# Fourteen pairs of expert chunks as seven block products instead of eight, in the second matmul of a PEER layer

## The chip, the core and the metric

The kernel runs on one core of one Trainium2 chip. The metric is the device time of that core in microseconds (us). A measurement is the median of several executions, and the traced execution has its own time.

The engines are named as in the profile: PE is TensorE (matmuls), PEld its weight loads, DVE is VectorE, ACT is ScalarE, POOL is GpSimd, and SP is SyncE, whose queue issues nearly all DMA loads. Each engine takes its instructions in the order in which they stand. An instruction that waits for a semaphore holds everything behind it on its engine.

## The reference, cut to what matters

```python
def reference(x, c, ...):                       # one layer: 256 tokens, width 1024
    mod = jax.nn.silu(c) @ ada_w + ada_b         # shift1, scale1, gate1, shift2, scale2, gate2
    ...                                          # two attention groups, w_out; x = x + g1 * y
    h2 = rmsnorm(x, norm2_g) * (1.0 + sc2) + sh2
    x = x + g2 * peer(h2, peer_wq, peer_subkeys, peer_u, peer_v)
    return rmsnorm(x, final_g)

def peer(h, wq, subkeys, u_tab, v_tab):          # 16384 experts of one neuron each
    ...                                          # product keys: 8 heads x 16 experts a token, gates by softmax
    a = h . u_tab[ids]                           # first expert matmul
    w = gates * gelu(a)
    return w . v_tab[ids]                        # second expert matmul
```

The kernel does not gather the experts. It computes all 16384 of them densely, as 128 chunks of 128 experts: with G the gates of the chosen experts spread over all experts (zero elsewhere), the second matmul is y = (G * gelu(h2 u^T)) v, of shape 256 x 16384 by 16384 x 1024.

## The kernel before, in words

All matmuls of the heavy part run as three products of split operands. A float32 operand is split into `hi`, its rounded part (an ACT copy to fp32r), and `lo`, the rest (a subtraction). `mm3` issues hi·hi, hi·lo and lo·hi into one PSUM bank (lines 130 to 133).

The work comes as a list of units, `order`, one unit of 128 x 1024 values each. For each unit `load` issues a DMA of 512 KB on SP's queue into a `raw` tile, and `split` makes `hi` on ACT and `lo` on POOL (kind "b") or DVE (kind "c"). `unit()` hands out the next unit, and prepares `lead[0]` units ahead in the program (1 here). In the last part of the kernel there are 3 `raw`, 4 `hi` and 3 `lo` tiles, used in turn. So the load of a unit waits until the unit three places before it in `raw` has been split, and a `lo` waits until TensorE has used the one three places before it.

- **First expert matmul.** 128 u chunks (24 matmuls of 256 columns each), with gelu. The results of 36 of them lie in `GA`, and the rest in `GB`, one cell of 256 tokens for each chunk. Beside 89 of them the gates are spread by one-hot matmuls (`gp`), 64 rounds.
- **Second expert matmul.** It follows without a gap. For each chunk i, `gated(i)` splits cell i into `wx` (3 tiles: ACT makes its hi half, DVE its lo half), `unit()` brings v chunk i, and `give` issues 4 products, one for each token tile T and half f of the width: 12 matmuls of 512 columns into the four PSUM banks `yp[T][f]`. The last 3 chunks are issued product by product, so that the banks become ready one after another. Two u chunks (126 and 127) stand between chunk 124 and these three.
- **Gate 2.** Its sum over the 8 row blocks of `ada` stands in the program from chunk 90 on, but the tile framework's scheduler places the loads and the sums early. They read into `GA` cells that are used up, not into `raw` (lines 859 to 873). The row then goes through DRAM (`g2d`) to be broadcast.
- **End.** y times gate 2, plus the residual stream `x1`, RMSNorm, and the store.

The order of instructions on each engine is set by the framework's scheduler, which orders them by priority and by its own estimates.

Of the kernel before, what the change touches and what calls it, by code (L numbers as in the profile page):

```python
# [15 lines left out]
D = 1024  # L16
S = 256
# [5 lines left out]
BIG = 1e30  # L23
LOW = -3e38
AHEAD = 36
BESIDE = 90
LEAD = 1
LATE = 5
E2AT = 0
HOLD = 1  # L30
GATE2 = 90
ENDLEAD = 2
LAST = 3
FG0 = (("p", 0, 512), ("p", 512, 1024))
# [36 lines left out]
def body(tc, xT, cols, ada, w_in, e2, w_out, wq, sk, u, v, fg, const, dil, out):  # L71
    nc = tc.nc
    with ExitStack() as top:
# [15 lines left out]

        def split(i, raw, eng):  # L90
            hi = room(i, "hi", F32R, *HIB)
            nc.scalar.activation(hi, raw, AF.Copy)  # L92
            lo = room(i, "lo", F32R, *LOB)
# [17 lines left out]
        order += [(v[i], "c") for i in range(AHEAD + BESIDE - 1)]  # L111
        for i in range(AHEAD + BESIDE - 1, NKEY - LAST):
            order += [(u[i + 1], "c"), (v[i], "c")]
        order += [(u[i], "c") for i in range(NKEY - LAST + 1, NKEY)]
        order += [(v[i], "c") for i in range(NKEY - LAST, NKEY)]
        ready = []
        loaded = []
# [57 lines left out]
        with ExitStack() as pre:  # L175
# [593 lines left out]
        def cell(i, t0, t1):  # L769
            return GA[:, i, t0:t1] if i < AHEAD else GB[:, i - AHEAD, t0:t1]  # L770
# [58 lines left out]
        with tc.tile_pool(name="py", bufs=1, space=bass.MemoryType.PSUM) as PY:  # L829
# [1 line left out]
            W = {}  # L831

            def gated(i):
                if i < done:
                    w = cell(i, 0, S)
                else:
                    ps = u_chunk(i)
                    w = WK.tile([128, S], F32, tag="w", name="w", bufs=1)
                    nc.scalar.activation(w, ps[:, :S], AF.Gelu)
                    nc.vector.tensor_mul(w, w, cell(i, 0, S))  # L840
# [14 lines left out]
            def used(n):  # L855

                return GA[:, 4 * n:4 * n + 4, :].rearrange("p a t -> p (a t)")

            def gate2(k):

                if k == 0:
                    nc.sync.dma_start(used(0), row(sild))
                if k < 8:
                    nc.sync.dma_start(used(1 + k % 2), ada[(40 + k) * 128:(41 + k) * 128, :])
                if k:
                    raw, c = used(1 + (k - 1) % 2), C_ADAB + 40 + k - 1
# [9 lines left out]
            for i in range(NKEY - LAST):  # L876
                gated(i + 1)
                if i >= GATE2 and (i - GATE2) % 3 == 0 and (i - GATE2) // 3 < 9:
                    gate2((i - GATE2) // 3)
                hl = unit()  # L880
                for T in range(2):
                    for f in range(2):
                        give(i, hl, T, f)

            lead[0] = ENDLEAD
            for i in range(NKEY - LAST + 1, NKEY):
# [6 lines left out]


            ys, scr = [used(T) for T in range(2)], used(2)
            g2b, fgb = used(3), used(4)
            x1 = [used(5 + T) for T in range(2)]
            for dst, src in ((g2b, row(g2d)), (x1[0], x1d[0]), (x1[1], x1d[1]), (fgb, row(fg))):
                nc.sync.dma_start(dst, src)
# [102 lines left out]
```

## Time and profile before

| what | value |
|---|---|
| median of 3 runs | 994.31 us (993.05 to 996.11) |
| the profiled execution | 996.15 us, span of its trace 994.3 us |
| PE busy | 965.2 us, 97% of the span |
| DVE busy | 724.4 us (73%) |
| ACT busy | 545.9 us (55%) |
| mean granted TensorE clock | 0.978 of full speed |

A matmul's busy time overlaps with that of the next, so the cost of one is read from the distance of the starts. A DVE or ACT instruction's time likewise overlaps a little with the next on its engine.

### The profile page before, as it was taken

The page shows a single profiled execution, that of the slowest core. Times are in us where ns is not written, and L with a number is a line of the kernel's source. Part 1 is how long each engine was busy: PE and PEld are TensorE (multiplying, and loading weights), DVE is VectorE, ACT ScalarE, POOL GpSimd, SP SyncE. Part 2 cuts the span into 40 slices and gives each one's busy share as a digit, 9 for nine tenths or more (in the row PEclk, how much of TensorE's full clock was granted, in tenths as well). Part 3 has the DMA queues.
Part 4 walks back from the last instruction along what each step waited for, and adds up shares of the span by engine and source line. Part 5 has one row for each costly group of instructions (what it writes and reads, how often), then busy time and mean ns, then how long its engine had stood idle before and what let it go on. Part 6 is the DMA issues. An engine that isn't in the chain of part 4 may idle for free.

```text
span 994.3 us, 17364 instructions
## 1 busy us (share of the span) xinstructions
PE 965.2 (97%) x6315; PEld 879.2 (88%) x6315; DVE 724.4 (73%) x1683; ACT 545.9 (55%) x1010; POOL 439.9 (44%) x201
## 2 busy tenths in 40 slices
PE   7998989999999999999999999999999999999996
PEld 4886978899999999999999999888888888888885
DVE  5969867799994577788888887677555555555555
ACT  4465556645444666666666666554545555444553
POOL 4458337587888777777777777000000000000002
PEclk8899869999999999999999999999999999999998
DMA  9687646555554555555555555688766666566662
GB/s 344 251 302 274 213 191 222 159 162 157 186 178 147 153 166 169 154 166 168 162 162 168 165 157 168 206 288 277 244 196 191 196 195 196 191 191 193 191 215 79
DMA packets 53398, 193.76 MB, mean 195 GB/s; under 512 B 5816, under 2 KB 6080, under 8 KB 53184
## 3 DMA queue, kind: packets, MB, share of 16 engines
q1 hardware_dynamic: 52672, 191.59, 59.8%
q8 instruction: 49, 0.80, 0.3%
q10 hardware_dynamic: 576, 1.05, 0.3%
q14 instruction: 37, 0.30, 0.1%
q0 software_dynamic: 64, 0.01, 0.0%
HBM read 190.52 MB, written 2.11 MB: 194 GB/s over the span
## 4 chain that ended last, share of the span: by engine, by line
PE 80%; DVE 1%; POOL 1%; ACT 1%; issue 1%; DMA 0%; POOLq 0%; ACTq 0%
PE ps L131 14%; PE ps L132 14%; PE ps L133 14%; PE y L131 12%; PE y L132 12%; PE y L133 11%; PE gp L805 3%; PE scp L660 1%; DVE xgxd L563 0%; DMA raw<-in_u 0%; POOL GA L917 0%; POOL lo L94 0%; DVE x_s L478 0%; POOL GA L923 0%; ACT xge2s L562 0%
## 5 line engine op out<-in xcount | busy, mean ns | idle before, releaser
L94 POOL TENSOR_TENSOR lo<-raw,hi 128x1024 fp32r<-128x1024 f32 x165 | 401.8, 2437 | 178.2 <-ACT hi L92 96.5
L92 ACT ACTIVATE hi<-raw 128x1024 fp32r<-128x1024 f32 x304 | 320.0, 1055 | 166.3 <-issue 63.6
L131 PE MATMUL ps<-h2h,hi 128*128 128x256 f32 x1128 | 320.4, 284 | 0.8 <-ACT GB L824 0.8
L132 PE MATMUL ps<-h2l,hi 128*128 128x256 f32 x1128 | 319.1, 283 | 0.0
L133 PE MATMUL ps<-h2h,lo 128*128 128x256 f32 x1128 | 318.8, 283 | 0.0
L94 DVE TENSOR_TENSOR lo<-raw,hi 128x1024 fp32r<-128x1024 f32 x139 | 171.9, 1237 | 136.5 <-issue 109.2
L131 PEld LDWEIGHTS ps<-h2h,hi 128*128 128x128 f32 x1128 | 216.2, 192 | 1.5 <-ACT GB L824 1.2
L132 PEld LDWEIGHTS ps<-h2l,hi 128*128 128x128 f32 x1128 | 216.4, 192 | 0.0
L133 PEld LDWEIGHTS ps<-h2h,lo 128*128 128x128 f32 x1128 | 216.2, 192 | 0.0
L131 PE MATMUL y<-hi,wx 128*128 128x512 f32 x512 | 199.2, 389 | 0.0
L133 PE MATMUL y<-hi,wx 128*128 128x512 f32 x512 | 199.2, 389 | 0.0
L132 PE MATMUL y<-lo,wx 128*128 128x512 f32 x512 | 199.2, 389 | 0.0
L873 POOL DMA_DIRECT2D g2d<-g2r x1 | 0.6, 617 | 317.0 <-ACT g2r L872 317.0
L791 DVE SCALAR_TENSOR_TENSOR gi<-iotaG,iT,gT 128x256 fp32r<-128x256 f32 x256 | 113.9, 477 | 31.5 <-PE gp L805 31.5
L131 PEld LDWEIGHTS y<-hi,wx 128*128 128x128 f32 x512 | 96.1, 188 | 20.3 <-ACT wx L843 0.2
L133 PEld LDWEIGHTS y<-hi,wx 128*128 128x128 f32 x512 | 96.1, 188 | 20.1 <-DVE wx L844 0.2
L132 PEld LDWEIGHTS y<-lo,wx 128*128 128x128 f32 x512 | 96.1, 188 | 19.6
L843 ACT ACTIVATE wx<-GB 128x256 fp32r<-128x256 f32 x90 | 37.7, 419 | 118.8 <-PE y L133 118.8
L808 DVE TENSOR_TENSOR gp<-gp,gl 128x512 f32<-128x512 f32 x64 | 44.6, 698 | 8.9 <-ACT gl L807 7.3
L788 DVE TENSOR_TENSOR jm<-iotaG,jT 128x512 fp32r<-128x512 f32 x64 | 43.6, 681 | 1.6 <-ACT iotaG L777 1.6
L811 ACT ACTIVATE GB<-gp 128x368 f32<-128x368 f32 (+31 forms) x64 | 21.3, 333 | 37.5 <-DVE gp L808 37.5
L209 DVE CUSTOM_DVE_ANT_0 araw<-araw,silb,col 128x1024 f32<-128x1024 f32 x24 | 41.4, 1738 | 0.1
(214 smaller groups left out, 1232.9 us busy)
## 6 DMA issues: line engine op xcount, KB each, us to landing
raw<-in_u SPq DMA_DIRECT2D x128, 512.0 KB, 3.6
raw<-in_v SPq DMA_DIRECT2D x128, 512.0 KB, 4.3
araw<-in_ada SPq DMA_DIRECT2D x20, 1024.0 KB, 6.2
raw<-in_w_in SPq DMA_DIRECT2D x24, 512.0 KB, 5.8
raw<-in_wq SPq DMA_DIRECT2D x16, 512.0 KB, 3.6
raw<-in_w_out SPq DMA_DIRECT2D x8, 512.0 KB, 6.4
GA<-in_ada SPq DMA_DIRECT2D x8, 512.0 KB, 5.3
e2s<-in_e SPq DMA_DIRECT2D x1, 1536.0 KB, 10.0
```

Source lines behind the costliest of these rows:

```text
L92: nc.scalar.activation(hi, raw, AF.Copy)
L94: ins = eng.tensor_tensor(lo, raw, hi.bitcast(F32), op=OP.subtract)
L131: nc.tensor.matmul(ps, wh, ah, start=first, stop=False)
L132: nc.tensor.matmul(ps, wh, al, start=False, stop=False)
L133: return nc.tensor.matmul(ps, wl, ah, start=False, stop=last)
L209: nc.vector.tensor_tensor_reduce(raw, raw, silb, 1.0, init, OP.mult, OP.add, m)
L788: nc.vector.tensor_tensor(jm, iotaG[:, None, :].to_broadcast([128, 4, 128]), jT[:, t0:t0 + 4, None].to_broadcast([128, 4, 128]), op=OP.is_ ...
L791: nc.vector.scalar_tensor_tensor(gi[:, t, :, :], iotaG[:, None, :].to_broadcast([128, 2, 128]), iT[:, t0 + t:t0 + t + 1], gT.bitcast(F32)[ ...
L805: nc.tensor.matmul(gp[:, t, :, :], jm[:, t, :], gi[:, t, :, :], start=True, stop=True)
L808: nc.vector.tensor_tensor(gp[:, :, 0, :], gp[:, :, 0, :], gl, op=OP.add)
L811: nc.scalar.activation(GB[:, m:, t0:t0 + 4], gv[:, done:, :], AF.Copy)
L843: nc.scalar.activation(wh, w, AF.Copy)
```

## The change

Two neighbouring chunks form a block matrix product: the 256 tokens are two blocks (T), the 256 experts two blocks (chunk e), the 1024 columns two blocks (f). Written out it has eight block products. Winograd's form of Strassen's scheme needs seven, at the price of sums of blocks on both sides:

- Every seventh chunk from 20 to 111 begins a pair, 14 pairs in all (`seven`). The other chunks are done as before, 5 between two pairs. Seven products of 3 matmuls of 512 columns take the place of eight.
- `pair_load` loads both v chunks (2 x 512 KB) into blocks 0 to 3 of `bl`, which is the first part of `GA`. DVE forms the sums of blocks: `pair_t13` (one subtraction of 1024 columns a partition) and `pair_t24` (two of 512). The blocks are split in four parts of 2, 1, 2 and 2 blocks (kind "s"), on ACT and DVE, and use the `hi` and `lo` tiles like any unit.
- `pair_s` forms four sums of gate blocks (128 columns each) on DVE, and splits them (`sx`). `pair_a` splits the two cells as they are (`wxh`, `wxl`).
- Products that go into one output block alone are added into `yp`. Four others have PSUM banks of their own (`P[1]`, `P[5]`, `P[6]`, `P[7]`) over all 14 pairs. After the last pair `fold` adds them up, multiplies them by gate 2 and adds them to the residual stream `x1`: 12 DVE instructions of 512 columns.
- Gate 2 is summed beside chunks 0 to 15. Its 8 row blocks are units of `order` now (kind "g"), one after every second v chunk, and take `raw` tiles.
- All 128 u chunks come before the second matmul (BESIDE 92, HOLD 3), three of them behind the last one-hot round instead of one. The loads of gate 2's row, `x1` and the final gain are issued behind the last pair in the program.

```diff
+        for i in plan:
+            order += [(p, "s") for p in range(4)] if i in seven else [(v[i], "c")]
+            if i < 16 and i % 2:
+                order.append((ada[(40 + i // 2) * 128:(41 + i // 2) * 128, :], "g"))
...
+                if kind == "s":
+                    ready.append(split(i, parts[order[i][0]], nc.vector))
+                    continue
+                if kind == "g":
+                    ready.append(load(i))
+                    continue
...
+            bl = GA[:, 0:16, :].rearrange("p (b a) t -> p b (a t)", a=2)
+            parts += [bl[:, 0:3:2, :], bl[:, 3:4, :], bl[:, 4:6, :], bl[:, 6:8, :]]
...
+            def pair_load(i):
+                for e in range(2):
+                    nc.sync.dma_start(bl[:, 2 * e:2 * e + 2, :], v[i + e].rearrange("p (f c) -> p f c", f=2))
+
+            def pair_t13(i):
+
+                nc.vector.tensor_tensor(bl[:, 4:6, :], bl[:, 1:4:2, :], bl[:, 0:2, :], op=OP.subtract)
...
+                for ops in (((a(0, 0), P[1]), (a(1, 0), yp[0][0])), ((s_(4), yp[0][1]),), ((s_(1), P[5]), (s_(3), P[7])),
+                            ((s_(2), P[6]), (a(1, 1), yp[1][0]))):
+                    hl = unit()
+                    for n, (w, o) in enumerate(ops):
+                        own = any(o is t for t in P.values())
+                        mm3(o, w[0], w[1], hl[0][:, n, :], hl[1][:, n, :], own and i == seven[0], own and i == seven[-1])
...
+            def gate2(k):
+                raw, c = unit(), C_ADAB + 40 + k
+                nc.vector.tensor_tensor_reduce(raw, raw, silr, 1.0, col[:, c:c + 1], OP.mult, OP.add, mod[:, 5, k:k + 1])
...
+                p1, r, c12, c21, c22 = (bl[:, n, :] for n in range(5))
+                nc.scalar.activation(p1, P[1], AF.Copy)
+                nc.vector.tensor_add(r, P[6], p1)
+                nc.vector.tensor_add(c12, P[5], r)
+                nc.vector.tensor_add(c21, P[7], r)
+                nc.vector.tensor_add(c22, P[7], c12)
+                for n, c in enumerate((p1, c12, c21, c22)):
+                    fs = slice(n % 2 * 512, (n % 2 + 1) * 512)
+                    nc.vector.tensor_mul(c, c, g2b[:, fs])
+                    nc.vector.tensor_add(x1[n // 2][:, fs], x1[n // 2][:, fs], c)
```

What the scheduler makes of it is seen in the order on the engines, at three places.

**SP's queue where gate 2 is loaded.** Before, the blocks of `ada` go to `GA_1996`, and the v chunks alone use `raw`:

```order
L87 DMA raw_8525<-in_v 128x1024
L87 DMA raw_8546<-in_v 128x1024
L864 DMA GA_1996<-in_ada 128x1024
L87 DMA raw_8567<-in_v 128x1024
L87 DMA raw_8588<-in_v 128x1024
L864 DMA GA_1996<-in_ada 128x1024
```

Now every third `raw` tile takes a block of `ada`. The rows are v2, v3, a block, v4, v5, a block, the first chunk of the first pair (`GA_1996`), v6, v7, a block, v8:

```order
L88 DMA raw_8460<-in_v 128x1024
L88 DMA raw_8470<-in_v 128x1024
L88 DMA raw_8491<-in_ada 128x1024
L88 DMA raw_8505<-in_v 128x1024
L88 DMA raw_8515<-in_v 128x1024
L88 DMA raw_8536<-in_ada 128x1024
L878 DMA GA_1996<-in_v 128x1024
L88 DMA raw_8550<-in_v 128x1024
L88 DMA raw_8560<-in_v 128x1024
L88 DMA raw_8581<-in_ada 128x1024
L88 DMA raw_8595<-in_v 128x1024
```

The load of an even chunk (v4, v6, v8) now waits for the split of the even chunk just before it, since the three `raw` tiles serve two chunks and a block of `ada`.

**DVE at a pair in the middle.** Before, one `lo` and one `wx` alternate through the whole second matmul:

```order
L94 TENSOR_TENSOR lo_9243<-raw_9239,hi_9241 128x1024
L844 TENSOR_TENSOR wx_9236<-GB_4125,wx_9236 128x256
L94 TENSOR_TENSOR lo_9264<-raw_9260,hi_9262 128x1024
L844 TENSOR_TENSOR wx_9257<-GB_4125,wx_9257 128x256
L94 TENSOR_TENSOR lo_9285<-raw_9281,hi_9283 128x1024
```

Now, at the third pair (chunks 34 and 35): `lo` of its first part (lo_9196), of its second (lo_9215), the lo halves of its cells (`wxl`), `lo` of its third part (lo_9225), the `wx` of the chunk behind the pair, `pair_t13` of the next pair (L882), `lo` of its fourth part (lo_9232), and `lo` of the two chunks behind it:

```order
L98 TENSOR_TENSOR lo_9196<-GA_1996,hi_9195 128x1024
L895 TENSOR_TENSOR sr_9503<-GB_4125,sr_9503 128x128
L98 TENSOR_TENSOR lo_9215<-GA_1996,hi_9214 128x512
L905 TENSOR_TENSOR wxl_9190<-GA_1996,wxh_9189 128x256 x2
L98 TENSOR_TENSOR lo_9225<-GA_1996,hi_9224 128x1024
L852 TENSOR_TENSOR wx_9211<-GB_4125,wx_9211 128x256
L882 TENSOR_TENSOR GA_1996<-GA_1996 128x1024
L98 TENSOR_TENSOR lo_9232<-GA_1996,hi_9231 128x1024
L98 TENSOR_TENSOR lo_9244<-raw_9241,hi_9243 128x1024
L98 TENSOR_TENSOR lo_9261<-raw_9258,hi_9260 128x1024
```

`pair_t13` of the next pair stands ahead of the last part of this one, and reads the next pair's two loads. On SP's queue those two loads wait for the first and the second row shown here (lo_9196 and lo_9215). This order holds at the second to the thirteenth pair. At the first pair the next `pair_t13` stands three units later, and at the last there is none.

**DVE behind the last pair.** Now: `lo` of the two chunks behind the pair, the 12 instructions of `fold` as one block with a single `wx` in it, and then `wx` and `lo` of the third chunk behind the pair. Before there was only the alternation shown above.

```order
L98 TENSOR_TENSOR lo_11015<-raw_11012,hi_11014 128x1024
L98 TENSOR_TENSOR lo_11047<-raw_11044,hi_11046 128x1024
L950 TENSOR_TENSOR GA_1996<-P6_8889,GA_1996 128x512
L852 TENSOR_TENSOR wx_11041<-GB_4125,wx_11041 128x256
L951 TENSOR_TENSOR GA_1996<-P5_8890,GA_1996 128x512
L952 TENSOR_TENSOR GA_1996<-P7_8891,GA_1996 128x512
L953 TENSOR_TENSOR GA_1996<-P7_8891,GA_1996 128x512
L956 TENSOR_TENSOR GA_1996<-GA_1996 128x512 x2
L957 TENSOR_TENSOR GA_1996<-GA_1996 128x512 x2
...
L852 TENSOR_TENSOR wx_11062<-GB_4125,wx_11062 128x256
L98 TENSOR_TENSOR lo_11068<-raw_11065,hi_11067 128x1024
```

The 12 instructions now stand between the splits of two chunks.

## Rows read from the trace of the kernel before

**Rows 1.** Windows of the second matmul: busy us (count) per engine, clock, DMA share, GB/s.
```profile
631.40:700.00 68.60, 68.60 (x305) 56.82 (x305) 48.43 (x66) 35.05 (x50) 0.00 (x0) 1.00 0.83 274
700.00:950.00 250.00, 250.00 (x1105) 206.97 (x1104) 143.78 (x185) 126.57 (x186) 0.62 (x1) 1.00 0.65 197
950.00:985.90 35.90, 35.86 (x181) 30.06 (x179) 22.03 (x29) 15.83 (x25) 2.98 (x3) 1.00 0.45 141
```

**Rows 2.** The chain that ended last, share of the span by engine.
```profile
PE 80%; DVE 1%; POOL 1%; ACT 1%; issue 1%; DMA 0%; POOLq 0%; ACTq 0%
```

**Rows 3.** Timeline of PE: start us, us, engine, line, operation, tiles.
```profile
955.31 0.39 PE L131 MATMUL y<-hi,wx 128*128 128x512 f32 x1
955.53 0.39 PE L132 MATMUL y<-lo,wx 128*128 128x512 f32 x1
...
955.99 0.39 PE L131 MATMUL y<-hi,wx 128*128 128x512 f32 x1
```

**Rows 4.** Who waited for whom, 700 to 950: us in total, times, longest.
```profile
ACT wx L843 <- PE y L133: 113.2, 85, 1.4
DVE lo L94 <- issue: 97.0, 84, 1.3
```

**Rows 5.** Groups of instructions, 631.4 to 985.9: busy us, mean ns | idle before.
```profile
L94 DVE TENSOR_TENSOR lo<-raw,hi 128x1024 fp32r<-128x1024 f32 x128 | 156.8, 1225 | 130.7 <-issue 109.2 <-ACT hi L92 15.3 <-PE ps L133 3.0
...
L867 DVE CUSTOM_DVE_ANT_0 GA<-GA,col 128x1024 f32<-128x1024 f32 x8 | 10.3, 1284 | 7.6 <-DMA GA<-in_ada 6.8 <-DVE wx L844 0.9
```

**Rows 6.** Timeline of DVE in the second matmul.
```profile
955.34 1.23 DVE L94 TENSOR_TENSOR lo<-raw,hi 128x1024 fp32r<-128x1024 f32 x1 [1.00 <-issue]
...
956.48 0.42 DVE L844 TENSOR_TENSOR wx<-GB,wx 128x256 fp32r<-128x256 f32 x1
```

**Rows 7.** DMA issues by line, windows 640 to 660 and 660 to 680: KB, us to landing.
```profile
raw<-in_v SPq DMA_DIRECT2D x7, 512.0 KB, 4.7
GA<-in_ada SPq DMA_DIRECT2D x3, 512.0 KB, 5.7
...
raw<-in_v SPq DMA_DIRECT2D x7, 512.0 KB, 5.0
```

**Rows 8.** Loads into `raw`, from 700 to 950.
```profile
DMA to landing us min/median/max: 3.4/4.3/6.1
```

**Rows 9.** Timelines of ACT and of DVE: a split whose load came late.
```profile
689.59 1.06 ACT L92 ACTIVATE hi<-raw 128x1024 fp32r<-128x1024 f32 x1 [1.17 <-DMA raw<-in_v]
690.68 1.23 DVE L94 TENSOR_TENSOR lo<-raw,hi 128x1024 fp32r<-128x1024 f32 x1 [0.67 <-ACT hi L92]
```

**Rows 10.** DVE at the end of the kernel: instructions of 512 columns.
```profile
980.65 0.69 DVE L908 TENSOR_TENSOR GA<-y,GA 128x512 f32<-128x512 f32 x1 [0.60 <-PE y L133]
981.38 0.69 DVE L909 TENSOR_TENSOR GA<-GA 128x512 f32<-128x512 f32 x1
981.99 0.68 DVE L908 TENSOR_TENSOR GA<-y,GA 128x512 f32<-128x512 f32 x1
```

**Rows 11.** The row of gate 2 to DRAM: KB, us to landing.
```profile
g2d<-g2r POOLq DMA_DIRECT2D x1, 4.0 KB, 3.7
```

**Rows 12.** Timeline of PE, earlier in the kernel, behind idle time.
```profile
97.31 0.91 PE L404 MATMUL sp<-k,q 64*128 64x256 f32 x5 [1.02 <-DVE mn L417]
130.04 0.48 PE L452 MATMUL tp<-cst,os 128*128 128x128 f32 x1 [3.19 <-ACT os L467]
159.15 0.44 PE L452 MATMUL tp<-cst,os 128*128 128x128 f32 x2 [1.31 <-ACT os L467]
```

**Rows 13.** Windows there; the clock stands after POOL's busy time.
```profile
98.00:100.00 2.00, 2.00 (x12) 1.60 (x10) 2.00 (x3) 0.84 (x1) 1.81 (x2) 0.56 0.72 289
104.00:106.00 2.00, 2.00 (x15) 2.00 (x14) 2.00 (x9) 1.42 (x6) 0.00 (x0) 0.73 0.80 236
130.00:132.00 2.00, 1.96 (x9) 1.97 (x10) 0.17 (x1) 2.00 (x8) 0.00 (x0) 0.50 0.68 188
160.00:162.00 2.00, 2.00 (x20) 2.00 (x19) 1.05 (x4) 1.39 (x3) 1.21 (x1) 1.00 0.04 8
```

More of the change, by code (lines that the diff above doesn't have):

```diff
@@ L29 @@
 E2AT = 0
-HOLD = 1
-GATE2 = 90
+HOLD = 3
+SEVEN = (20, 7, 118)
 ENDLEAD = 2
@@ L91, in split @@
             hi = room(i, "hi", F32R, *HIB)
+            lo = room(i, "lo", F32R, *LOB)
+            if raw.shape[-1] == 512:
+                n = raw.shape[1]
+                hi, lo = (t[:, :n * 512].rearrange("p (n c) -> p n c", n=n) for t in (hi, lo))
             nc.scalar.activation(hi, raw, AF.Copy)
-            lo = room(i, "lo", F32R, *LOB)
             ins = eng.tensor_tensor(lo, raw, hi.bitcast(F32), op=OP.subtract)
@@ L110, in body @@
         order += [(u[i], "b") for i in range(AHEAD + BESIDE)]
[L111 to L114, printed above, removed]
+        seven = [i for i in range(*SEVEN[:1], SEVEN[2]) if (i - SEVEN[0]) % SEVEN[1] == 0]
+        plan = [i for i in range(NKEY - LAST) if i - 1 not in seven]
+        parts = []
+        for i in plan:
+            order += [(p, "s") for p in range(4)] if i in seven else [(v[i], "c")]
+            if i < 16 and i % 2:
+                order.append((ada[(40 + i // 2) * 128:(41 + i // 2) * 128, :], "g"))
         order += [(v[i], "c") for i in range(NKEY - LAST, NKEY)]
@@ L833, in gated @@
             def gated(i):
[L834 to L840, printed above, removed]
+                w = cell(i, 0, S)
                 wx = WK.tile([128, 2, S], F32R, tag="wx", name="wx", bufs=WXB)
@@ new lines, in pair_s @@
+            def pair_s(i):
+                a11, a21, a12, a22 = (cell(i + e, T * 128, (T + 1) * 128) for e in range(2) for T in range(2))
+                sr = WK.tile([128, 4, 128], F32, tag="w", name="sr", bufs=1)
+                for o, x, y, op in ((0, a21, a22, OP.add), (2, a11, a21, OP.subtract), (1, sr[:, 0, :], a11, OP.subtract),
+                                    (3, a12, sr[:, 1, :], OP.subtract)):
+                    nc.vector.tensor_tensor(sr[:, o, :], x, y, op=op)
+                sx = WK.tile([128, 2, 4, 128], F32R, tag="gi", name="sx", bufs=2)
+                nc.scalar.activation(sx[:, 0], sr, AF.Copy)
+                nc.vector.tensor_tensor(sx[:, 1], sr, sx[:, 0].bitcast(F32), op=OP.subtract)
+                AS[i] = sx
@@ new lines, in pair_a, with pair_products, a, s_ @@
+            def pair_a(i):
+                wx = [WK.tile([128, 2, S], F32R, tag="wx", name="wx" + x, bufs=WXB) for x in "hl"]
+                for e in range(2):
+                    nc.scalar.activation(wx[0][:, e, :], cell(i + e, 0, S), AF.Copy)
+                    nc.vector.tensor_sub(wx[1][:, e, :], cell(i + e, 0, S), wx[0][:, e, :].bitcast(F32))
+                W[i] = wx
+            def pair_products(i):
+                sx, wx = AS.pop(i), W.pop(i)
+                def a(e, T):
+                    return [t[:, e, T * 128:(T + 1) * 128] for t in wx]
+                def s_(n):
+                    return [sx[:, x, n - 1, :] for x in range(2)]
+                if not P:
+                    for n in (1, 6):
+                        P[n] = PY.tile([128, 512], F32, name=f"P{n}")
+                    for n in (5, 7):
+                        P[n] = PM.tile([128, 512], F32, tag="mm", name=f"P{n}")
+                for ops in (((a(0, 0), P[1]), (a(1, 0), yp[0][0])), ((s_(4), yp[0][1]),), ((s_(1), P[5]), (s_(3), P[7])),
[4 more added lines that the diff above has]
+                        mm3(o, w[0], w[1], hl[0][:, n, :], hl[1][:, n, :], own and i == seven[0], own and i == seven[-1])
@@ L870, in gate2 @@
+            silr = WK.tile([128, D], F32, tag="gi", name="silr", bufs=2)
+            nc.sync.dma_start(silr, row(sild))
+            def gate2(k):
+                raw, c = unit(), C_ADAB + 40 + k
+                nc.vector.tensor_tensor_reduce(raw, raw, silr, 1.0, col[:, c:c + 1], OP.mult, OP.add, mod[:, 5, k:k + 1])
+                if k == 7:
+                    gp = PM.tile([128, 512], F32, tag="mm", name="gp2")
                     nc.tensor.transpose(gp[0:8, 0:128], mod[:, 5, :], ident)
@@ L873, in gate2, with fold @@
                     nc.gpsimd.dma_start(g2d, g2r)
-            gated(0)
[L876 to L879, printed above, removed]
+            g2b, fgb = used(4), used(7)
+            x1 = [used(5 + T) for T in range(2)]
+            def fold():
+                p1, r, c12, c21, c22 = (bl[:, n, :] for n in range(5))
[8 more added lines that the diff above has]
+                    nc.vector.tensor_add(x1[n // 2][:, fs], x1[n // 2][:, fs], c)
+            gated(0)
+            todo = []
+            for n, i in enumerate(plan):
+                nxt = plan[n + 1] if n + 1 < len(plan) else NKEY - LAST
+                todo += [(n + 2 if j == 0 else max(n + 2, plan.index(p) - 3 + j), j, p) for p in seven
+                         if p == next((q for q in seven if q >= nxt), None) and (i in seven or i == 16) for j in range(4)]
+                for t in [t for t in todo if t[0] <= n + 1]:
+                    todo.remove(t)
+                    (pair_load, pair_t13, pair_t24, pair_s)[t[1]](t[2])
+                (pair_a if nxt in seven else gated)(nxt)
+                if i in seven:
+                    pair_products(i)
+                    if i == seven[-1]:
+                        for dst, src in ((g2b, row(g2d)), (x1[0], x1d[0]), (x1[1], x1d[1]), (fgb, row(fg))):
+                            nc.sync.dma_start(dst, src)
+                        fold()
+                    continue
                 hl = unit()
@@ L883, in body @@
                         give(i, hl, T, f)
+                if i < 16 and i % 2:
+                    gate2(i // 2)
             lead[0] = ENDLEAD
@@ L895, in body @@
             ys, scr = [used(T) for T in range(2)], used(2)
[L896 to L899, printed above, removed]
             ssq = WK.tile([128, 4], F32, name="fssq")
```

16 lines of the change are left out of this document (6 added, 10 removed).

## The prediction

> **What bounds the kernel now.** I read the windows of the second matmul first [rows 1]. From 631.4 to 985.9 PE is busy without a break at a granted clock of 1.00, while DVE is busy 143.8 us of 250 and ACT 126.6. The chain that ended last is PE for 80% of the span [rows 2]. So in this stage time is the number of matmuls times the distance of their starts. The timeline gives that distance: 0.227 us, 0.68 us for a product of three [rows 3], 2.72 us for a chunk of four products.
>
> The other engines wait for PE: ACT for a `wx` tile that PE has used, 113 us in 250, and DVE, whose `lo` finds no free tile, for 97 us [rows 4]. They have slack, but little lead. Three `lo` tiles let the splits run two units ahead of PE. A `lo` starts when PE has used the tile three units before, that is at the end of a chunk (955.34 [rows 6], with the next chunk's first matmul at 955.31 [rows 3]).
>
> **What it removes.** 14 pairs lose one product each: 14 x 0.68 = **9.5 us**, all on the path, if PE stays fed. The rest of this part asks whether it does.
>
> **Gate 2 through `raw` (loss 8.5).** The 3 tiles serve two v chunks and one block of `ada` in turn for chunks 0 to 15. The load of an even chunk waits for the `lo` of the even chunk before it. One round is: load, from issue to landing; hi and the step to `lo`, 1.09 (689.59 to 690.68) [rows 9]; `lo`, 1.23; 0.02 to the next issue. Loads landed in 4.3 us at one in 2.72 us [rows 8], in 4.7 at ten in 20 us, and in 5.0 where they were denser [rows 7]. Three in a round of almost 7 us is one in 2.3 us, between the first two: I take 4.5. A round is then 6.84 us, and PE uses its two chunks in 5.44, so each round costs 1.4. With time 0 at the first v matmul, `lo` of v2 ends at 2.4 (its tile comes free at 0), v4's at 9.25, where PE wants it at 11.1. v6's load is issued with three others within 3 us (v5, a block, the pair's first chunk), lands 1.9 later than alone, and its `lo` ends at 18.0 instead of 16.55: 1.5 late. v8 to v16 are five rounds: 5 x 1.4 = 7.0. Sum 8.5. In the kernel before the same blocks went past `raw`, and PE did not wait [rows 1]. The sums themselves (1.28 us each [rows 5]) fit into DVE's slack.
>
> Here one rule speaks against me. The Trainium skill, page "DMA: Bandwidth & Descriptors", section "Anatomy of one DMA — SWDGE (gpsimd) path", fits a DMA's time as 2.0 us plus its bytes at 436 GB/s. For 512 KB that is 3.2 us, an estimate from that page, for another issuing path than SP's. By it a round would be 5.5 us and this term almost nothing. The rows show no load into `raw` from 700 to 950 under 3.4, and half of them over 4.3 [rows 8], so I go by the rows; the lowest of them is a rival below.
>
> **The first pair (loss 1.6).** Its `sr` tile is one with `g2r`, so DVE waits there for gate 2's row to reach DRAM: the transpose stands behind chunk 15 on PE, and the DMA lands 3.7 later [rows 11]. Behind `sr` on DVE stand the splits of v19 and of the pair, and three `sr`/`sx` sets that the scheduler moved here (some 4 us). Laid out, v19 is just in time, and the parts come 0.2, 1.0 and 0.4 late.
>
> **The pairs 2 to 13 (loss 0.87 each, 10.4).** Time 0 is the start of the pair's first part on PE; the parts start at 0, 1.36, 2.04 and 3.40. DVE's `lo` of the second part needs the tile of the chunk before last, free at -2.69; it lasts 0.69 (512 columns [rows 10]) and ends at -2.0. Only then may SP issue the next pair's second load; at 4.3 it lands at 2.3. Loads are dense here (four in 5.3 us), so 4.3 is no high value. Meanwhile DVE does `wxl`, `lo` of the third part (tile free at 0.03) and a `wx`, until 1.5, and stands at `pair_t13`, which needs that load. It lasts like `lo`, two inputs of 1024 columns, 1.15 to the next start [rows 6]. So `lo` of the fourth part starts at 3.45 and ends at 4.68. PE wants it at its third matmul of that part, 3.40 + 0.454 = 3.85 (two hi matmuls stand ahead of it there), so with the semaphore it waits 0.87. The chunk behind the pair just fits: its `lo` ends at 5.83, wanted at 5.87. DVE catches up afterwards. Its work in a period is 5 x (1.15 + 0.34) for chunks, 4.1 for the parts, 0.7 for `wxl`, 2.4 for `pair_t13` and `pair_t24`, 1.6 for the small sums: 16.2 us of a period of 18.4, so it does not bound by itself, and each pair begins the same way. A pair thus costs 0.87 and saves 0.68. If the load lands at 3.4, DVE alone sets it and the wait is 0.1; at 5.0 it is 1.6.
>
> **`fold` (loss 4.1, and 3.1 for the clock).** 12 DVE instructions, 0.61 to 0.73 each from start to start [rows 10], are 7.9 us in one block, with one `wx`. It starts 0.3 behind the last pair's end. Two chunks are split ahead and give PE 5.44. `wx` and `lo` of the third come at 9.7, wanted at 5.67: 4.1 late, once. PE was idle so long only once in the rows: 3.19 us at 130, then the clock was 0.50 [rows 12, 13]. An idle 1.31 at 159 left it at 1.00; 1.02 at 97, with little work before, was followed by half clock until about 105, some 6.2 us. For `fold` I count one such stretch, 3.1 us; below it is nothing. For the 0.9 to 1.5 of the other waits I count none.
>
> **What costs nothing.** The two u chunks moved ahead (48 matmuls) are the same work; at the end, without them, `lo` of v127 starts when v124's tile is free and ends 1.26 later, wanted at 1.59, so that cover is not missed (otherwise 1 us). POOL splits them one a chunk, as it does the 126 others. ACT has half of its time free and takes 1.5 more splits a pair. The loads of `x1`, gain and gate row are issued long before the end in both kernels. The tail is the same.
>
> **Sum.** -9.5 + 8.5 + 1.6 + 10.4 + 4.1 + 3.1 = +18.2. Against the profiled execution's 996.15 us (span 994.3) that is 1014.3; that execution lay 1.8 above the median of the runs, so on the median it is 1012.5, and I say **1012**.
>
> **The rivals.**
> - Loads land fast (not slower). At 3.4 us everywhere, a round is 5.74: the first lateness falls away, and the later rounds cost 0.9 together. The pairs cost 0.1 each, 1.2; the first pair 1.0; `fold` 4.1, with the clock 7.2. Sum +0.8, or -2.3 if the clock holds: 992 to 995. For it speaks the lowest row; against it the median [rows 8] and the denser loads [rows 7]. It decides at a landing of about 3.5. By the 3.2 of that page it would come out about 1 us lower still.
> - The clean saving: the splits keep ahead of PE at every place, and only the 9.5 counts, 985. For it speaks DVE's free time on the average [rows 1]; against it that the waits arise from the order in three places, not from DVE's sum. The largest single one, `fold`, would have to be hidden by a lead of 4 us that three `lo` tiles don't hold.
> - Contention makes it heavier. With loads at 5.0 as around 670 [rows 7], a round is 7.34: 12 us for gate 2; the pairs 12 x 1.6 = 19; the first pair 2.2; `fold` 7.2. Sum +31: 1025.
>
> **Numbers.** My forecast 0.70 (its own range 1003 to 1019), fast loads 0.15, the clean saving 0.07, contention 0.08. A measurement of this kernel can tell about 0.3%, 3 us. Faster: the clean saving, and a part of the fast loads: 0.12. Within: 0.11. Slower: 0.77. For 8 in 10 the range takes in the fast loads, and stops short of contention's end: 992 to 1021.
>
> **What would show it.** If I am right, PE has idle time of about 1.4 us before every second chunk from v6 to v16, released by DVE `lo`, whose ACT hi waited for the load; `pair_t13` waits for a load by DMA, 0.8 us at each of 12 pairs, and PE for `lo` right behind it; PE waits once about 4 us for the `wx` and `lo` behind `fold`, with the clock down afterwards. PE issues 42 matmuls of 512 columns fewer. I would be wrong if loads into `raw` land in 3.5 us or less, if `pair_t13` starts without a wait, or if the rounds of gate 2 take 5.4 us.

## The result, and the profile after

The changed kernel takes 1022.43 us (median of 4 runs, 1015.87 to 1023.19) where the kernel before takes 993.68 beside it. The ratio is 1.0274, with an interval of 1.0245 to 1.0303: slower, by 24 to 30 us. The prediction said slower, by 18. Its range ended at 1021, so the measured median lies 1.4 us above it.

The profiled execution of the changed kernel took 1022.85 us, span 1020.9, which is 26.6 more than the span before. I cut it where the work changes: the second matmul begins (639.28), the first pair (701.30), the last pair (961.39, at the end of the second window), the end of the matmuls. The windows answer to [rows 1], with the same columns (PE, PEld, DVE, ACT, POOL, clock, DMA share, GB/s):

```profile
639.30:701.30 62.00, 57.47 (x243) 44.38 (x242) 43.42 (x67) 27.82 (x44) 0.62 (x1) 1.00 0.77 250
701.30:962.00 260.70, 245.36 (x1057) 197.69 (x1056) 210.28 (x311) 153.17 (x223) 0.00 (x0) 0.99 0.57 191
962.00:985.00 23.00, 19.81 (x81) 15.88 (x80) 19.84 (x29) 11.41 (x17) 0.00 (x0) 0.93 0.40 137
985.00:1012.00 27.00, 27.00 (x121) 22.21 (x119) 17.42 (x23) 11.69 (x19) 2.19 (x2) 1.00 0.39 117
```

Before, PE was busy without a break here. Now it is idle for 4.5, 15.3 and 3.2 us in the first three windows, while DVE's share has risen to 81% in the second and is below 90% everywhere. An engine that is busy 81% of the time is no bound by itself, so what is wanted is the place of each wait. The chain that ended last (before: [rows 2]) says which engines have come into it:

```profile
PE 67%; DVE 6%; DMA 6%; ACT 2%; issue 2%; POOL 1%; POOLq 0%; DVEq 0%; ACTq 0%; SPq 0%
```

**Beside gate 2.** The same chain, piece by piece (start, us, what), from 654 to 675:

```profile
654.18 1.07 ACT hi L97
...
655.28 1.24 DVE lo L98
...
656.53 3.45 DMA raw<-in_v
...
660.00 1.07 ACT hi L97
...
661.10 1.24 DVE lo L98
...
662.35 5.31 DMA raw<-in_v
...
670.03 4.61 DMA raw<-in_v
```

Load, hi, lo, load again: PE is no longer in the chain at all. That is the ring of three `raw` tiles. PE's timeline shows where it stands, at the first and the second matmul of every second chunk:

```profile
667.67 0.39 PE L147 MATMUL y<-hi,wx 128*128 128x512 f32 x1
668.79 0.50 PE L145 MATMUL y<-hi,wx 128*128 128x512 f32 x1 [0.74 <-ACT hi L97]
670.05 0.50 PE L146 MATMUL y<-lo,wx 128*128 128x512 f32 x1 [0.76 <-DVE lo L98]
...
675.77 0.50 PE L145 MATMUL y<-hi,wx 128*128 128x512 f32 x1 [0.18 <-ACT hi L97]
677.02 0.50 PE L146 MATMUL y<-lo,wx 128*128 128x512 f32 x1 [0.76 <-DVE lo L98]
```

Two chunks take 6.98 us here (668.79 to 675.77), and 5.44 without a wait. The whole stretch from 639.28 to 701.30 holds 240 matmuls of 0.227, 54.5 us, and takes 62.0: 7.5 lost.

**A pair in the middle.** The view of waits from 701.3 to 962 (us in total, times, longest), where [rows 4] had nothing of PE or PEld:

```profile
PEld P L146 <- DVE lo L98: 21.3, 14, 3.0
...
PE P L146 <- DVE lo L98: 15.3, 13, 2.6
DVE GA L882 <- DMA GA<-in_v: 14.8, 12, 2.6
```

L882 is `pair_t13`: it waits 12 times for a load, 1.23 us each, and PE waits 13 times for a `lo`. At the fifth pair (its first matmul is at 783.09) the timelines of SP, DVE and PE give the order of it:

```profile
780.11 1.35 SPq L878 DMA_DIRECT2D GA<-in_v  x2
```

```profile
780.41 0.69 DVE L98 TENSOR_TENSOR lo<-GA,hi 128x512 fp32r<-128x512 f32 x1
...
784.27 0.42 DVE L852 TENSOR_TENSOR wx<-GB,wx 128x256 fp32r<-128x256 f32 x1
786.02 1.22 DVE L882 TENSOR_TENSOR GA<-GA 128x1024 f32<-128x1024 f32 x1 [1.33 <-DMA GA<-in_v]
787.17 1.22 DVE L98 TENSOR_TENSOR lo<-GA,hi 128x1024 fp32r<-128x1024 f32 x1
```

```profile
786.72 0.39 PE L145 MATMUL y<-hi,wxh 128*128 128x512 f32 x1
788.44 0.50 PE L146 MATMUL P<-lo,sx 128*128 128x512 f32 x1 [1.34 <-DVE lo L98]
788.78 0.40 PE L147 MATMUL P<-hi,sx 128*128 128x512 f32 x1
```

The second of the two loads goes out when `lo` of the second part is done (780.41 and 0.69, so 781.1; the row of SP merges both issues). Some 4.8 us later it has landed, and `pair_t13` starts; `lo` of the fourth part stands behind it, and PE behind that. From pair to pair (start of one to start of the next, less 81 matmuls of 0.227) the first period loses 1.1 us, the second 4.4, the third to the thirteenth 0.6 to 1.9, on average 1.41.

**`fold`.** DVE's timeline behind the last pair, and PE's:

```profile
966.70 0.68 DVE L950 TENSOR_TENSOR GA<-P,GA 128x512 f32<-128x512 f32 x1
967.30 0.41 DVE L852 TENSOR_TENSOR wx<-GB,wx 128x256 fp32r<-128x256 f32 x1
...
973.04 1.28 DVE L957 TENSOR_TENSOR GA<-GA 128x512 f32<-128x512 f32 x2
974.24 0.41 DVE L852 TENSOR_TENSOR wx<-GB,wx 128x256 fp32r<-128x256 f32 x1
974.58 1.21 DVE L98 TENSOR_TENSOR lo<-raw,hi 128x1024 fp32r<-128x1024 f32 x1
```

```profile
971.59 1.07 PE L145 MATMUL y<-hi,wx 128*128 128x512 f32 x4
975.85 0.50 PE L146 MATMUL y<-lo,wx 128*128 128x512 f32 x1 [3.19 <-DVE lo L98]
...
977.41 0.63 PE L147 MATMUL y<-hi,wx 128*128 128x512 f32 x1
977.84 0.63 PE L146 MATMUL y<-lo,wx 128*128 128x512 f32 x1
```

The block of 12, with two `wx`, holds `lo` back by 7.9 us. PE issues the four hi·hi matmuls of the chunk first, stands for 3.19, and from 976.98 to 979.97 a matmul takes 0.43 instead of 0.227. The window there has the granted clock at half (1.2 GHz), for 3.0 us, after the idle 3.19:

```profile
976.98:979.97 2.99, 2.99 (x8) 2.34 (x7) 2.18 (x4) 0.89 (x2) 0.00 (x0) 0.50 0.85 258
```

From the last pair's start to the last matmul 5.1 us are lost.

### The profile page after: what moved, and what is told of

Read it like the earlier page. It is cut to its first block, busy times and chain, and to the rows that moved or that the text cites. A ratio compares the mean times of both kernels' runs of the same rounds, so it can differ in the third digit from the quotient of the medians.

```text
span 1020.9 us, 17470 instructions
## 1 busy us (share of the span) xinstructions
PE 967.0 (95%) x6273; PEld 871.6 (85%) x6273; DVE 805.4 (79%) x1833; ACT 574.8 (56%) x1053; POOL 444.3 (44%) x203
## 4 chain that ended last, share of the span: by engine, by line
PE 67%; DVE 6%; DMA 6%; ACT 2%; issue 2%; POOL 1%; POOLq 0%; DVEq 0%; ACTq 0%; SPq 0%
PE ps L145 13%; PE ps L146 13%; PE ps L147 13%; PE y L146 7%; PE y L147 7%; PE y L145 7%; DMA raw<-in_v 4%; DVE lo L98 3%; PE gp L819 3%; PE P L146 1%; ACT hi L97 1%; PE P L147 1%; PE scp L674 1%; PE P L145 1%; DMA raw<-in_u 1%
## 5 line engine op out<-in xcount | busy, mean ns | idle before, releaser
L98 POOL TENSOR_TENSOR lo<-raw,hi 128x1024 fp32r<-128x1024 f32 x167 | 406.5, 2436 | 181.0 <-ACT hi L97 98.2
L97 ACT ACTIVATE hi<-raw 128x1024 fp32r<-128x1024 f32 x276 | 289.8, 1058 | 193.9 <-issue 63.7
L98 DVE TENSOR_TENSOR lo<-raw,hi 128x1024 fp32r<-128x1024 f32 x109 | 133.3, 1236 | 40.2 <-ACT hi L97 32.0
L146 PE MATMUL y<-lo,wx 128*128 128x512 f32 x400 | 157.9, 395 | 6.8 <-DVE lo L98 6.7
L145 PE MATMUL y<-hi,wx 128*128 128x512 f32 x400 | 156.7, 393 | 0.9 <-ACT hi L97 0.9
L147 PE MATMUL y<-hi,wx 128*128 128x512 f32 x400 | 157.0, 393 | 0.0
L146 PEld LDWEIGHTS y<-lo,wx 128*128 128x128 f32 x400 | 75.8, 189 | 26.9 <-DVE lo L98 10.0
L145 PEld LDWEIGHTS y<-hi,wx 128*128 128x128 f32 x400 | 75.7, 189 | 18.1 <-ACT hi L97 2.1
L147 PEld LDWEIGHTS y<-hi,wx 128*128 128x128 f32 x400 | 75.8, 190 | 15.4
L98 DVE TENSOR_TENSOR lo<-GA,hi 128x1024 fp32r<-128x1024 f32 (+1 forms) x56 | 60.9, 1088 | 24.9 <-PE y L146 19.9
L97 ACT ACTIVATE hi<-GA 128x1024 fp32r<-128x1024 f32 (+1 forms) x56 | 52.8, 943 | 18.8 <-PE y L147 18.8
L851 ACT ACTIVATE wx<-GB 128x256 fp32r<-128x256 f32 x70 | 27.5, 410 | 60.2 <-PE y L147 58.9
```

The costliest lines, as they stand in the source:

```text
L145: nc.tensor.matmul(ps, wh, ah, start=first, stop=False)
L146: nc.tensor.matmul(ps, wh, al, start=False, stop=False)
L147: return nc.tensor.matmul(ps, wl, ah, start=False, stop=last)
```

## The experiments

The losses below are read in each kernel's trace as above. This is finer than the times, because executions differ ahead of the part that was changed (last section).

**Gate 2 out of the ring** (`a_gate2_own`).

```diff
-                order.append((ada[(40 + i // 2) * 128:(41 + i // 2) * 128, :], "g"))
...
+            g2t = [P0.tile([128, 8, S], F32, tag="h" + x, name="g2" + x) for x in "hl"]
...
+                nc.sync.dma_start(g2raw[k % 4], ada[(40 + k) * 128:(41 + k) * 128, :])
```

> The 8 blocks of ada for gate 2 no longer take raw tiles; they go into four tiles of their own (the room of h2, which nothing reads any more). Everything else is as in the changed kernel. In the changed kernel the stretch from the first v matmul (639.28) to the first pair (701.30) holds 240 matmuls at 0.227 us, 54.5, and takes 62.0: 7.5 us of waits. My theory (the ring of three raw tiles sets them): they go to below 1 us, and the time falls from 1022.4 by about 7, to 1015. Rival (the loads are simply too dense there, 32 in 62 us, whichever tiles they go to): the loads land as late as before, PE still waits 5 us or more, 1020 to 1022. Rival (DVE's eight sums of 1.28 us are what is too much): the same, 1020 to 1022.

Measured: 1008.58 us (1.0163 of before, 1.0145 to 1.0181). The stretch up to the first pair takes 54.6 and loses 0.1 instead of 7.5. The same eight loads and eight sums still stand there, and the loads even landed later (median 5.3 us into `raw` and 6.6 for the blocks of `ada`, against 4.4 and 4.5 in the changed kernel). So neither the density of the loads nor DVE's work was the cause. The ring was. The time fell by twice what I said. In its profiled execution the second matmul began 6.0 us earlier than in the changed kernel's, ahead of anything that was edited, and the pairs and `fold` lost 3.3 us less, which this edit doesn't explain. PE stood the same 3.19 us behind `fold`, but here the granted clock stayed at 1.00 afterwards (961 to 966).

**Two places for a pair's loads** (`b_two_sets`).

```diff
+            bl2 = P0.tile([128, 8, S], F32, tag="hh", name="bl2").rearrange("p (b a) t -> p b (a t)", a=2)
+            src = {i: (bl, bl2)[n % 2] for n, i in enumerate(seven)}
...
-                    nc.sync.dma_start(bl[:, 2 * e:2 * e + 2, :], v[i + e].rearrange("p (f c) -> p f c", f=2))
+                    nc.sync.dma_start(src[i][:, 2 * e:2 * e + 2, :], v[i + e].rearrange("p (f c) -> p f c", f=2))
```

> The two v chunks of a pair are loaded alternately into two places (the old one in GA, and one in the room of h2), so the loads of the next pair no longer wait until this pair's blocks are split. DVE does the same instructions in the same order. In the changed kernel the twelve periods after the second, third, ... thirteenth pair's start lose 4.4 us (second) and 1.41 us each (third to thirteenth), 19.9 in all. My theory (pair_t13 stands at a load that was issued too late): the load is issued 2 to 3 us earlier and pair_t13 starts without a wait; what is left is 0.15 us a pair, so the time falls by 18, to 1004. Rival (DVE has too much to do in a pair, 16 us of 18): no change, 1020 to 1023. Rival (the loads land later the denser they stand, and DMA is what sets it): pair_t13 still waits for most of it, 1014 to 1020.

Measured: 1003.84 us (1.0097, 1.0074 to 1.0119). DVE's timeline at its fifth pair (L885 is `pair_t13` here, first matmul at 775.25) has the same rows without the wait:

```profile
776.44 0.42 DVE L852 TENSOR_TENSOR wx<-GB,wx 128x256 fp32r<-128x256 f32 x1
776.77 1.22 DVE L885 TENSOR_TENSOR GA<-bl 128x1024 f32<-128x1024 f32 x1
777.91 1.22 DVE L98 TENSOR_TENSOR lo<-GA,hi 128x1024 fp32r<-128x1024 f32 x1
```

The twelve periods lose 3.0 us together instead of 20.0. The loads still land in 4.6 us (median from 720 to 960), only they are issued in time. DVE's volume is the same, so it was not what PE waited for.

**`fold` spread over the chunks behind it** (`c_fold_spread`).

```diff
-                        fold()
+                        folding = fold()
...
+                if i > seven[-1]:
+                    with tc.issue_after(done_i.ins):
+                        next(folding)
```

> The twelve DVE instructions of fold are held apart: one or two behind each of the chunks that follow the last pair, instead of one block. My theory (the block of 7.9 us stands ahead of one wx and lo): the wait of 3.2 us of PE behind the last pair and the half clock after it go, 5.1 us from 961.39 to the end of the matmuls falls below 1, and the time to 1017.5. Rival (the 12 instructions cost their time wherever they stand, since DVE is short of time there): 1020 to 1022.

Measured: 1016.13 us (1.0217, 1.0192 to 1.0242). From the last pair on nothing is lost (less than 0.1 instead of 5.1): the same 12 instructions, one or two to a chunk, fit between the splits. The pairs, which this edit leaves alone, lost 3.3 us more than in the changed kernel: at the fifth and the eleventh PE stood 1.80 and 1.84 us, half clock followed, and these two periods lost 3.7 us each.

**All three** (`d_all_three`). The three edits together, with gate 2 in two tiles instead of four.

> All three at once: gate 2 in two tiles of its own, two places for the loads of a pair, fold spread out. My theory: 7 + 18 + 4.6 less, 1022.4 - 29.6 = 992.8 by the sum from the changed kernel; from the kernel before, 993.7 less the 9.5 of the 14 products, plus 1.1 for the first pair, 1.8 that is left at the others, 0.8 for the moved u chunks and 0.5 behind the last pair: 988.4. I expect 990, not slower than the kernel before. Rival (the pairs cost by DVE's volume or by the density of the loads): 1005 or more.

Measured: 988.48 us (0.9965, 0.9950 to 0.9980), 9 runs: a little faster than the kernel before, by 0.2 to 0.5%. The second matmul takes 342.5 us from its first matmul to its last, where the kernel before takes 348.3 (354.0 with its two u chunks): 9.5 saved, 0.6 lost at the first pair and 2.9 at the other twelve.

**The load of `x1`** (`e_x1_late`).

```diff
-            x1 = [used(5 + T) for T in range(2)]
+            x1 = [used(5), GB[:, 68:72, :].rearrange("p a t -> p (a t)")]
```

> From the changed kernel: the second half of x1 (512 KB) gets another place, cells of GB that come free after chunk 107, so that its load no longer stands in SP's queue right behind the two loads of the third pair (719.95 there). DVE's order is the same. My theory (that load shared the DMA engines with the pair's second load and made it land later): the period of the second pair, 22.83 us in the changed kernel, becomes like the others, 19.8, so 3.0 us less, 1019.4. Rival (the second pair is late for a reason of its own, for instance the gate sums behind gate 2's row): the period stays at 22.5 to 23, no change. The other periods should lose 1.4 each as before.

Measured: 1018.84 us (1.0258, 1.0227 to 1.0290), a step in the right direction that the two intervals don't separate. SP's queue at the second pair in the changed kernel, then the time to landing of its two loads (least, median, most), then the latter here:

```profile
718.45 1.46 SPq L878 DMA_DIRECT2D GA<-in_v  x2
719.95 0.43 SPq L974 DMA_DIRECT2D GA<-x1d  x1
```

```profile
DMA to landing us min/median/max: 3.9/4.6/5.2
```

```profile
DMA to landing us min/median/max: 4.3/4.4/4.5
```

The second period loses 1.6 us here, and 4.4 in the changed kernel. The difference is the wait (PE stood 2.58 us there, 1.28 here) and the half clock that followed the longer one. The load also went out 0.6 us later there against PE's start of the pair, so not all of it is the landing. That `x1` alone makes the difference is not shown. With `fold` spread, where its load also stands there, the load ahead of it took 6.35 us and the period lost 4.9; with gate 2 out of the ring it took 5.1, and the period lost only 1.9. And here the eleventh period, with no load of `x1` near, lost 3.7 behind an idle 1.78.

**No pairs** (`f_no_pairs`). `d_all_three` with SEVEN = (20, 7, 20).

> The kernel d_all_three without its pairs: all 128 chunks as before, gate 2 in two tiles of its own at the beginning, all u chunks ahead of the second matmul, y times gate 2 plus x1 at the end. My theory (only the pairs save anything; the other edits cost at most the 0.8 us by which the moved u chunks wait): like the kernel before, 993 to 994.5, and 5 to 6 us above d_all_three. Rival (gate 2 summed early, or the u chunks ahead, give part of the gain that d_all_three shows over the kernel before): below 992.

Measured: 993.64 us (1.0014, 0.9998 to 1.0030), 12 runs; its second matmul takes 348.2. So the gain of `d_all_three` comes from the pairs (5.2 us between these two medians), and the edits that are left here, to gate 2 and the u chunks, change nothing that can be measured.

**More pairs** (`h_every_sixth`, `i_every_fifth`, `j_every_fourth`). SEVEN = (20, 6, 118), (20, 5, 118) and (20, 4, 118) in `d_all_three`: 17, 20 and 25 pairs.

> d_all_three with a pair at every sixth chunk, 17 pairs instead of 14, four chunks between two. DVE's work in a period, by the prediction's count, is 8.8 for the pair and 4 x 1.49 for the chunks, 14.8 us of a period of 15.7. My theory: it just fits, each pair loses 0.2 as in d_all_three and saves 0.68, so three more pairs give 1.4 us: 987.1. Rival (DVE without reserve falls behind and does not catch up in four chunks): the later periods lose 0.5 or more each, 993 or more.

Measured: 988.77 us (0.9961, 0.9940 to 0.9981), 10 runs. Each period loses 0.2. The second matmul is 0.9 us shorter than with 14 pairs (341.6), which the times can't show.

> d_all_three with a pair at every fifth chunk, 20 pairs, three chunks between two. DVE's work in a period is now 8.8 + 3 x 1.49 = 13.3 us, PE's 36 + 21 matmuls, 12.9. My theory (here DVE's sum becomes the bound, which it is not in the changed kernel): the period is 13.3 or a little more, each pair loses at least 0.4, and the time is 988 to 992, no better than with 14 pairs. Rival (DVE's sum is not the bound even here, since its instructions overlap a little): 986 or less.

Measured: 984.56 us (0.9922, 0.9897 to 0.9947), 5 runs, the fastest of all. My theory was wrong here: each pair still loses only 0.2 (13.15 a period), and the second matmul takes 339.3.

> d_all_three with a pair at every fourth chunk, 25 pairs, two chunks between two. In i_every_fifth DVE was busy 138.5 us of 140 (760 to 900), with 13.16 us a period; one chunk less a period takes 1.49 from DVE, which leaves 11.5, while PE needs 24 + 21 matmuls, 10.2. My theory (DVE's sum bounds from here on): the period is 11.5 or more, each pair loses 1.3 and saves 0.68, some 15 us more than no pairs at all (993.6), 1004 to 1010. Rival (DVE's sum is smaller than its busy time says, as at every fifth chunk): each pair still loses 0.2, 981 to 984.

Measured: 1003.01 us (1.0098, 1.0082 to 1.0114). The period is 11.38 us, and from the sixth on each pair loses 1.15. The windows from 760 to 900 of the kernels with 14, 20 and 25 pairs, one fence each:

```profile
760.00:900.00 140.00, 139.74 (x610) 113.12 (x608) 120.24 (x181) 88.79 (x127) 0.00 (x0) 1.00 0.61 198
```

```profile
760.00:900.00 140.00, 140.00 (x609) 112.72 (x608) 138.51 (x216) 91.47 (x139) 0.00 (x0) 1.00 0.63 202
```

```profile
760.00:900.00 140.00, 138.38 (x557) 99.61 (x556) 140.00 (x222) 93.46 (x137) 0.00 (x0) 1.00 0.61 185
```

DVE goes from 86% over 99% to full. At 99% PE still does not wait for it more than 0.2 a pair; at full it does, and a pair then costs more than the 0.68 that it saves. Only here is DVE's sum the bound, as my theory had it; the time is 1 us under its range.

**The block sums on POOL** (`k_fourth_pool`, `l_fifth_pool`). The first of three lines that change alike:

```diff
-                nc.vector.tensor_tensor(bl[:, 4:6, :], src[i][:, 1:4:2, :], src[i][:, 0:2, :], op=OP.subtract)
+                nc.gpsimd.tensor_tensor(bl[:, 4:6, :], src[i][:, 1:4:2, :], src[i][:, 0:2, :], op=OP.subtract)
```

> j_every_fourth with the block sums of v (pair_t13, pair_t24) on POOL, which has nothing else to do in this stage. It takes 2.4 us off DVE in each period. The nearest rows for POOL's own time are its lo in the first matmul (2.44 us for 1024 columns) and 1.46 us for 512 at the end, together 5.3 us a period of 10.2. My theory: DVE then has 9.1 us in 10.2, and each pair loses 0.2 to 0.4, 981 to 985. Rival (POOL slows DVE while both work, or the sums come too late for the split of the third part): 990 or more.

> i_every_fifth with the block sums of v on POOL. The 0.2 us that each pair still loses in i_every_fifth come behind pair_t13, which stands ahead of the split of the fourth part on DVE. My theory: without it there the 0.2 go, 20 x 0.2 = 4 us less, 981. Rival (the 0.2 have another cause, or POOL's sums come late): 984 or more.

Measured: 1060.78 us (1.0693, 1.0671 to 1.0714) and 1042.89 us (1.0502, 1.0478 to 1.0526): each pair loses 3.5 and 3.15 us. My theory was wrong in both; the last section shows why.

**One load instead of two** (`m_one_load`).

```diff
-                for e in range(2):
+                for e in range(i != seven[0], 2):
                     nc.sync.dma_start(bl[:, 2 * e:2 * e + 2, :], v[i + e].rearrange("p (f c) -> p f c", f=2))
```

> The changed kernel, but from the second pair on the first of a pair's two chunks is not loaded; its place keeps the first pair's values, so the output lacks 13 v chunks. The second load stands where it stood, behind the split of the second part, and DVE's order at the third to the thirteenth pair is the same. In the changed kernel that load lands 4.7 to 4.9 us after its issue where the prediction took 4.3, and each of these pairs loses 1.41 us where the prediction said 0.87. Theory 1 (the load shares the DMA engines with the one issued 1 us ahead of it): alone it lands in 4.0 us or less, and a pair loses 0.6 or less. Theory 2 (a load of 512 KB takes that long behind the raw loads anyway): it lands in 4.6 us or more, and the loss stays at 1.3 to 1.5.

This kernel leaves out the first chunk of 13 pairs. Measured: 1005.37 us (1.0126, 1.0101 to 1.0151). Landing times of the pairs' loads from 745 to 960, in the changed kernel and here:

```profile
DMA to landing us min/median/max: 3.7/4.6/5.0
```

```profile
DMA to landing us min/median/max: 3.4/3.5/4.3
```

Alone the load lands 1.1 us sooner, and the third to the thirteenth pair lose 0.44 us each instead of 1.41. The loads into `raw` beside it land as before (median 4.0 in the changed kernel, 4.1 here), so it is not the smaller traffic on the whole. This is theory 1. In the changed kernel the first load of a pair takes as long as the second (median 4.6 for each), so the later one doesn't just stand behind the earlier; no run here has the first load alone.

## Why the prediction was right, and where its size was off

The direction and the places were right: the three waits that the prediction laid out are the ones that the trace shows, and each went away when its own cause was taken away. The size was 10 us short. Its terms, against the profiled execution:

| term | predicted | measured |
|---|---|---|
| 14 products less | -9.5 | -9.5 |
| gate 2 through `raw` | +8.5 | +7.5 |
| the first pair | +1.6 | +1.1 |
| pairs 2 to 13 | +10.4 | +20.0 |
| `fold`, and the clock after it | +4.1, +3.1 | +5.1 together |
| what costs nothing | 0 | +1.0 |
| ahead of the change | - | +1.3 |

This makes 26.5 of the 26.6 by which the spans differ. The pairs alone were 9.6 short; the total came nearer by luck, since gate 2, the first pair and `fold` were sized 3.6 too high together.

**What it removes** was right: two kernels that differ in the pairs alone, and where these hardly wait, lie 5 us apart in the times and 5.7 in the trace, which is 9.5 less 0.6 and 2.9 of waits, within 0.3.

**Gate 2 through `raw`** was right in mechanism and nearly in size. Between the first matmuls of v10, v12, v14 and v16 (668.79, 675.77, 682.38, 689.12) a round takes 6.8 us on average; the prediction had 6.84.

**The pairs 2 to 13** are the term that was mis-sized, 0.87 us each where 1.41 was measured, and 4.4 at the second. The order of the steps was right, to within 0.1 us up to the issue of the load: `lo` of the second part ends 2.0 before the pair's start, `pair_t13` takes 1.15 to the next, PE wants the `lo` at +3.86. The step that failed is "at 4.3 it lands at 2.3". I took the median of all loads into `raw` before [rows 8] and called it no high value. At the fifth pair the load took 4.8: +0.5. It goes out 1 us behind another load of the same size, and the run without that other one shows that this is what it pays for. To this come 0.26 that the prediction left out: from PE's idle 1.34 to the next start it is 1.49 (786.72 to 788.44, less 0.227), and the first matmul after the wait takes 0.34. Over the third to the thirteenth pair the load took 4.55 on average; its 0.25 and the 0.26 bring 0.87 to 1.38, of 1.41. At the second pair a load of `x1` stood right behind in the queue, which the prediction had dismissed ("issued long before the end in both kernels") without asking what else is in flight there. That pair lost 3 us more than the others, the half clock after it counted in; how much of this is the load of `x1` is open.

The Trainium skill, page "DMA: Bandwidth & Descriptors", section "Anatomy of one DMA — SWDGE (gpsimd) path", would have it at 3.2 us for 512 KB by its fit, an estimate for a DMA from another path. The load that stood alone, 3.4 at the least and 3.5 in the median, comes near it. With another one 1 us ahead, 4.6 is the median, which that fit does not give: it is a floor here, and no value for a load in a group. The rival "loads land fast" fell for this reason. The rival "contention" came near in its sum for the pairs (19) and was wrong for gate 2 (12). Its 19 is luck: it took a landing of 5.0, where 4.55 was measured, and had neither the 0.26 nor the clock.

**`fold`** was 4.1 late as laid out (975.85 is 4.0 behind the start that PE would have made). PE had three more hi·hi matmuls to do in this time, so the lateness cost 3.35. The clock's term was too large: I took the long stretch of [rows 12, 13], 6.2 us, and the half clock here lasted 3.0. It is no fixed price: behind the same idle 3.19 there was none in `a_gate2_own`, and 13 matmuls at half rate in `m_one_load`, where the changed kernel has 7.

**What costs nothing** was nearly so: 0.8 lies between the last one-hot matmul and the second matmul, where PE twice stands 0.4 us for a `GB` cell, beside 0.2 in the tail. The kernel without pairs shows neither in its time.

**The first pair** lost 1.1 for 1.6.

## What to carry to other kernels

Work that fits on the average still costs if it is put in the wrong place: a shared buffer ring, a load issued one step late and a block of 12 instructions took 33 us from an engine whose helper was busy 81%, and moving them, with not one instruction less, turned a loss of 29 us into a gain of about 4 (8 with more pairs). When a load's issue hangs on a buffer, size its landing by the loads that go out within a microsecond or two of it, not by the median of the stage. Ahead of moving work to an idle engine, look for what the two engines share.

## What was not expected of the hardware

**POOL holds DVE up.** With the block sums on POOL and a pair at every fourth chunk, POOL's rows and DVE's, from the two timelines:

```profile
800.12 2.52 POOL L883 TENSOR_TENSOR GA<-bl 128x1024 f32<-128x1024 f32 x1 [5.57 <-DVE lo L98]
803.86 2.14 POOL L887 TENSOR_TENSOR GA<-bl,GA 128x512 f32<-128x512 f32 x1 [1.23 <-DVE lo L98]
806.08 2.15 POOL L888 TENSOR_TENSOR GA<-bl,GA 128x512 f32<-128x512 f32 x1
```

```profile
798.82 1.22 DVE L98 TENSOR_TENSOR lo<-GA,hi 128x1024 fp32r<-128x1024 f32 x1
...
800.29 3.43 DVE L98 TENSOR_TENSOR lo<-GA,hi 128x1024 fp32r<-128x1024 f32 x1
803.64 3.45 DVE L98 TENSOR_TENSOR lo<-raw,hi 128x1024 fp32r<-128x1024 f32 x2
807.01 2.31 DVE L98 TENSOR_TENSOR lo<-bl,hi 128x1024 fp32r<-128x1024 f32 x1
```

A `lo` takes 1.22 us, and 3.43 when it starts behind a sum on POOL: the 2.35 until POOL is done (802.64), and about its own 1.2. The Trainium skill, page "SBUF — State Buffer", section "Who interferes with whom", says that a DVE instruction with two inputs in SBUF contends with a GpSimd instruction that reads SBUF, and calls the port pair that they share an exclusive lock. The trace agrees. From 760 to 900 DVE was busy 139.31 of 140 us here, so it did not wait for late sums: its own `lo` took longer, 2.36 us on average for the 26 that read `GA`. With a pair at every fifth chunk the same `lo` took 3.35 (at 806.10). My theory of these two runs had left this out; it stood only among the rivals of the first.

**The clock ahead of the change.** Up to the end of the first matmul, PE has the same instructions in the same order in all these kernels, yet executions differ there by 6 us. Windows from 130 to 150 in the changed kernel and in the one with gate 2 out of the ring:

```profile
130.00:150.00 20.00, 17.61 (x88) 14.89 (x89) 11.89 (x33) 11.33 (x27) 6.29 (x3) 0.66 0.42 168
```

```profile
130.00:150.00 20.00, 20.00 (x153) 18.60 (x152) 15.57 (x38) 12.53 (x29) 9.93 (x4) 0.93 0.60 227
```

In the one TensorE was granted 0.66 of its clock on the mean, so most of the time the lower level of 1.2 GHz, and did 88 matmuls; in the other it was 0.93, mostly 2.4 GHz, and 153. This window alone does not set where the second matmul begins: with two places for a pair's loads the clock was 0.91 in it, and the second matmul began at 637.41, between the two (633.26 and 639.28). What decides between the two levels I did not find out. In the second matmul too the same wait did not always have the same price: behind an idle 1.80 the fifth period with `fold` spread lost 3.7 us, with the clock at 0.50 (787.7 to 790.7), and behind an idle 1.81 the first with gate 2 out of the ring lost 2.3, with the clock at 1.00 (693.9 to 699). It is why a difference of a few us is better read in the stage that was changed, and wait by wait.
